# Ordering the column-strip matmuls of the modulation weights: all four of a row tile in a row, the later piece first

## The chip, the cores and the metric

One core of one Trainium2 chip. The metric is device microseconds of one execution of the program; the median of 3 runs of the kernel before is 2380.18 us (2373.62 to 2383.07).

## The reference

Two transformer blocks on 256 tokens of 1024 features, in float32. The first block mixes sparse attention with a gated linear recurrence in chunks and ends with a feed-forward layer. The second has two layers on a sequence x and a context of 256 tokens; each layer scales, shifts and gates its norms and branches by nine modulations, which a vector c (and c_ctx for the context) gives. The change touches these:

```python
for l in range(DEPTH_2):
    mod_x = (jax.nn.silu(c) @ w_ada[l] + b_ada[l]).reshape(bn, 1, N_MOD, d)
    mod_c = (jax.nn.silu(c_ctx) @ w_ada[l] + b_ada[l]).reshape(1, 1, N_MOD, d)
    h_x = _half_ffn(h_x, norm_g[l, 0], mod_x[:, :, 0], mod_x[:, :, 1], mod_x[:, :, 2], ffn1_up[l], ffn1_down[l])
    h_c = _half_ffn(h_c, norm_g[l, 0], mod_c[:, :, 0], mod_c[:, :, 1], mod_c[:, :, 2], ffn1_up[l], ffn1_down[l])
...
```

Here w_ada[l] is 1024 x 9216, and c and c_ctx are one row each.

## The kernel before, in words

Activations lie feature-major (128 features of a tile in the partitions, tokens along the free axis). A large product is three matmuls, because values and weights are split in a high and a low part: `gemm` (L360 to L366) issues high x high (L364), low x high (L365) and high x low (L366) for each row tile. A `Stream` (L333) brings weights in: `load` (L342, its DMA at L349) takes one of a few raw buffers of 128 x 1024 floats (512 KB), `get` (L352) splits such a piece by ScalarE (L356) and by VectorE or GpSimd (L357). All weight loads go through one queue, SP's, which issues them in order and waits when the next one's buffer is still in use. The buffers of a pool are given out in turn, in the order in which the program text asks for them.

The modulations of a layer are made by `Ada.step` (L1150 to L1182) in five parts: four of two modulations each, and one of the last modulation alone. The two vectors (x and context) and 30 zero columns are the stationary operand `sc` of 128 x 32, and the weights are the moving operand, in plain float32. The 1024 rows are eight row tiles (k). In the first four parts a row tile has 2048 columns, which come as two pieces `r` of 1024 columns, and each half of a piece (512 columns) is multiplied by one matmul. Four such matmuls, j = 0 to 3, write four strips of 32 partitions of one PSUM tile, so they use four different groups of 32 columns of the systolic array; j = 0, 1 read the first piece and j = 2, 3 the second:

```python
for j in range(4):
    te.matmul(pt[j * 32:j * 32 + 32], adac[:, k], w[j], start=k == 0, stop=k == KD - 1)   # L1163
if k < KD - 1:
    yield
```

In the fifth part a row tile is one piece of 1024 columns, and a strip has 256 columns. Two layers have 64 row tiles of two pieces and 16 of one, 320 strip matmuls; each shows as two records in the profile (two passes of a float32 matmul). After the eighth row tile four transposes (L1171) and VectorE turn the part into its place.

`step` is a generator: the program takes one row tile at a time between other work. The stream `st_c` with three raw buffers carries the pieces, and it carries also the feed-forward weights of the context in the second block's first layer (`Ffn.group`, L443, which calls `tick` after each hidden tile: two pieces for the gate and up columns, then two modulation pieces), since this part of the context does not wait for block 1 and runs beside it. Block 1 takes ten row tiles ahead of its first norm (`E0`) and then one for each column tile of its projections (L621 on); its own weights come through another stream with two raw buffers. Layer 1's modulations go on beside block 1's output projection and beside the joint feed-forward layers of x and context, after 1200 us, there through three raw buffers of their own.

The order in which instructions stand on an engine is not the order of the program text: the tile framework's scheduler takes, of the instructions that are free by their dependencies, the one that its own model finds ready. So strips of two pieces of a row tile can stand apart, with other matmuls between them, and strips of different row tiles can stand together. Matmuls of one row tile do not depend on each other.

Of the kernel before, what the change touches and what calls it, by code (L numbers as in the profile page):

```python
# [17 lines left out]
PSUM = bass.MemoryType.PSUM  # L18
DRAM = bass.MemoryType.DRAM

D = 1024
KD = 8
# [7 lines left out]
# the work of the three mixers: projections, and then what goes beside the units of either attention (a group for each).  # L30
# q, k, v, c, u: projections; V, C, U: what one of their tiles still needs; b: bias; t: a step from outside; s: statistics
# [106 lines left out]
def stat(w, c0, c1):  # L138
    """[K, M] columns c0:c1 as stationary pieces of 128 columns: [M/128, 128, K/128, 128]."""
    w = np.asarray(w)[:, c0:c1]  # L140
    k, m = w.shape
    return np.ascontiguousarray(w.reshape(k // 128, 128, m // 128, 128).transpose(2, 1, 0, 3))


def movp(w):
    """[1024, 512] as moving pieces of 2 row tiles: [4, 128, 2, 512]."""
    w = np.asarray(w)
    return np.ascontiguousarray(w.reshape(4, 2, 128, w.shape[1]).transpose(0, 2, 1, 3))


def upw(a, b):
    """gate and up columns, interleaved by tile: [22, 2, 128, 8, 128]."""
    return np.ascontiguousarray(np.stack([stat(a, 0, FF), stat(b, 0, FF)], 1))


def per_piece(g):
    """column tiles in a down piece of g row tiles"""
    return 1 if g > 4 else 2 if g > 2 else 4


def dnw(w, groups):
    """[2816, 1024]: for each group of row tiles and few column tiles, [128, g, n * 128], one after another."""
    w = np.asarray(w).reshape(NF, 128, 8, 128)
    out, f0 = [], 0
    for g in groups:
        nd = per_piece(g)
        out.append(np.ascontiguousarray(w[f0:f0 + g].reshape(g, 128, 8 // nd, nd * 128).transpose(2, 1, 0, 3)).ravel())
        f0 += g
    return np.concatenate(out)


def adaw(w):
    """[1024, 9216]: pieces [72, 128, 1024] in the order of their use: two modulations at a time, in four parts"""
    w = np.asarray(w).reshape(8, 128, 9216)
    out = []
    for i in range(4):
        a = w[:, :, i * 2048:(i + 1) * 2048]
        for k in range(8):
            out.append(a[k, :, 0:1024])
            out.append(a[k, :, 1024:])  # L180
    for k in range(8):
        out.append(w[k, :, 8192:])
    return np.ascontiguousarray(np.stack(out))
# [82 lines left out]
def build(tc, A, O, dbg=(), stop=None):  # L266
    nc = tc.nc
    v, s, g, te, sy = nc.vector, nc.scalar, nc.gpsimd, nc.tensor, nc.sync
# [64 lines left out]
    class Stream:  # L333
# [8 lines left out]
        def load(self, src, a, b, i=0):  # L342
            """a piece as it is; other rings than the usual one take the i-th of many at once"""
            if i < self.nr:
                r = tl(self.raw, [128, 1024], tag="r")
            else:
                r = f32(tl((self.h, self.l)[i % 2], [128, 1024], F32R, tag="hl"[i % 2]))
            rv = r[:, 0:a * b].rearrange("p (a b) -> p a b", a=a)
            self.q.dma_start(rv, src)  # L349
            return rv  # L350
# [9 lines left out]
    def gemm(pt, w, m0, m1, xs):  # L360
        """pt += columns m0:m1 of a split stationary piece, over the tiles xs of (hi, lo)"""
        n = len(xs)
        for k in range(n):
            te.matmul(pt, w[0][:, k, m0:m1], xs[k][0], start=k == 0, stop=False)  # L364
            te.matmul(pt, w[0][:, k, m0:m1], xs[k][1], start=False, stop=False)  # L365
            te.matmul(pt, w[1][:, k, m0:m1], xs[k][0], start=False, stop=k == n - 1)  # L366
# [13 lines left out]
    def squares(pp, ps, src, n, late=0, nb=3, scale=None):  # L380
        """sums [128, n / 128] of the squares of src(k), k = 0..7, token-major; the last, late of them, are summed
        by the tensor engine alone"""
        nt = n // 128
        ss = ps(nt)

        def total(sq, first, last):
            for t in range(nt):
                te.matmul(ss[:, t:t + 1], sq[:, t * 128:(t + 1) * 128], ones[:, 0:1], start=first and t == 0, stop=last,
                          skip_group_check=True)

        early = KD - late
        for k in range(KD):
            sq = tl(pp, [128, n], tag="sq", bufs=nb) if k or not early else tl(pp, [128, n], tag="sa", bufs=1)
            s.activation(sq, src(k), AF.Square, scale=scale(k) if scale else 1.0)
            if k == 0:
                acc = sq
            elif k < early:
                g.tensor_tensor(acc, acc, sq, op=OP.add)  # L398
            if k >= early:
                total(sq, k == 0, k == KD - 1)  # L400
            elif k == early - 1:
                total(acc, True, not late)
        return ss

    def stats(pp, ps, src, n, rs, late=0, nb=3):
        """rs [128, n / 128] = 1 / rms of src(k), k = 0..7, token-major"""
# [4 lines left out]
    def rms(pp, ps, src, n, out, late=0, rs=None):  # L411
        """out(k, bc): bc [128, n] is 1 / rms of src(k), k = 0..7, along the columns"""
# [12 lines left out]
    def norm_split(pp, ps, src, n, yh, yl, sc, sh=None, late=0, rs=None):  # L425
        """src * rstd * sc(k) + sh(k) in parts yh, yl"""
# [57 lines left out]
    # ================= block 1 =================  # L484
    def block1(ps, early, ready):
# [8 lines left out]
        # rope tables from the positions  # L494
# [48 lines left out]
        for _ in range(E0):  # L543
            next(early, None)
        with ExitStack() as e:
# [10 lines left out]
            def rope_in(dst, nh, cos, sin, rows=128, pp=pp):  # L556
                """dst [rows, nh, 64] in place"""
# [9 lines left out]
            # token-major queries, then keys and values  # L567
# [57 lines left out]
            # feature-major: receptance, keys, values, low-rank inputs  # L625
# [30 lines left out]
            # compressed keys and values  # L656
# [143 lines left out]
        with ExitStack() as e:  # L800
# [16 lines left out]
            # decay: log w = -e^-0.5 sigmoid(w0 + tanh(w_lat) w2); running sums in each chunk  # L817
# [21 lines left out]
            def head_rstd(sq, scale, eps, floor, neg):  # L839
                """sum of sq over the 64 features of a head -> (.)^-0.5, over the features of the head, in PSUM"""  # L840
# [22 lines left out]
            # negated, normalised keys  # L863
# [15 lines left out]
            # the bonus r . k_mod r_k, over v  # L879
# [9 lines left out]
            # A~ = -kk P_{t-1}, R~ = r P: [pair, token tile, which, token]  # L889
# [20 lines left out]
            # token-major A~, B^, K^, V  # L910
# [20 lines left out]
            # Gram blocks, transposed [j, i]  # L931
# [28 lines left out]
            # (I - L)^-1 by substitution: a partition is (parity of the columns, head, chunk)  # L960
# [92 lines left out]
            # group norm over a head, bonus, gate  # L1053
# [31 lines left out]
    def block1_out(ps, st, before_last):  # L1085
        mix = b1mix
        xr = lambda k: res[:, k, 0:T]
# [1 line left out]
        with ExitStack() as e:  # L1089
# [20 lines left out]
            # the scale of the output norm, and of the norm that follows it on its result  # L1110
# [11 lines left out]
    # ================= block 2 =================  # L1122
# [14 lines left out]
    class Ada:  # L1137
        """modulations of a layer, feature-major: M [128, 9, 8, (x, ctx)], and GS = g (1 + scale) of its three norms"""
# [11 lines left out]
        def step(self, i, st, ps):  # L1150
# [4 lines left out]
            for k in range(KD):  # L1155
# [6 lines left out]
                for j in range(4):  # L1162
                    te.matmul(pt[j * 32:j * 32 + 32], adac[:, k], w[j], start=k == 0, stop=k == KD - 1)  # L1163
# [20 lines left out]
    # each table's rope rows, with the norm's gains (and the queries' 1/8) folded in  # L1184
# [22 lines left out]
    def qkn(pp, src, nh, seg, t, tab, hl):  # L1207
        """heads [128, nh, 64]: norm, rope, split into hl [128, nh, 2, 64]"""
# [80 lines left out]
    def in_v(l, st, pp, ps, yh, yl, segs, kvs, tab):  # L1289
        """values and keys; returns what is left to do for the keys, a token tile at a time"""  # L1290
# [27 lines left out]
    def in_qc(l, st, pp, ps, yh, yl, seg, t0, tab, QC):  # L1318
        """queries; returns what is left to do, a token tile at a time"""
# [24 lines left out]
    def attend(pp, ps, pst, pso, Q, nh, keys, vals, kvof, mh, ml, bias=None, tick=None):  # L1344
        """keys: [(KH, KL)], vals(i, kt, kv) -> [128, 64]; mh, ml [128, nh / 2, 256]"""
# [56 lines left out]
    class Bias:  # L1402
        """the neighbourhoods' bias and mask of (head, token tile) units, in parts, made some units ahead"""
# [22 lines left out]
    def in_u(l, st, pp, ps, yh, yl, c0, mh, ml):  # L1426
        """pooled columns; returns what is left to do, half of the groups at a time"""
# [34 lines left out]
    def mixer(l, seg, st, qp, side, ps, pin, pst, pso, yh, yl, c0, segs, kvs, tab, mixt, orders, out=True, tick=None, extra=None):  # L1462
        """projections of the sequences segs, attention, pooling and output projection of seg; its columns start at c0"""
# [63 lines left out]
    def norm_mod(l, j, seg, pp, ps, yh, yl, late=0, rs=None):  # L1527
        """modulated norm j of a sequence's residual"""
# [12 lines left out]
    def out_proj(l, seg, st, ps, mixt, half):  # L1541
        """one half of the mixed rows, two column tiles a step"""
# [38 lines left out]
    # the context of block 2's first layer does not wait for block 1: its pools lie at the other end of the memory  # L1581
# [53 lines left out]
    # x, first layer  # L1635
# [37 lines left out]
    # both, to the second layer's projections; x goes ahead of the context at each norm  # L1673
# [79 lines left out]
```

## Time and profile before

| | |
|---|---|
| median of 3 runs | 2380.18 us |
| lowest and highest run | 2373.62 and 2383.07 us |
| span of the profiled execution (the only time given for it) | 2382.3 us |
| TensorE, matmuls | 2283.6 us busy, 96% |
| VectorE | 1374.2 us, 58% |
| ScalarE | 946.8 us, 40% |
| GpSimd | 361.0 us, 15% |
| strip matmuls (L1163) | 640 records, in two stretches: 12 to 545 us and 1206 to 1706 us |
| DMA | 376.25 MB, mean 158 GB/s |

The span is the time from the first to the last instruction of one execution that was profiled; the runs are timed without a profile. Busy time is time in which an engine had an instruction in it, whether it could have been shorter or not. A wait names what came last before the waiting instruction could start. In a timeline, equal instructions that follow each other are one line with a count, and the time of a matmul includes its way through the array, so that the next one starts before its end; what a matmul costs is read from the starts.

### The profile page before, as it was taken

How to read it: one execution, taken by the hardware profiler on the slowest of the kernel's cores; microseconds unless marked ns; L12 is line 12 of the kernel's file. 1: busy time of each engine (PE TensorE's matmuls, PEld its weight loads, DVE VectorE, ACT ScalarE, POOL GpSimd, SP SyncE). 2: the span in 40 equal slices, each digit the busy share in tenths (PEclk: the TensorE clock that was granted, in tenths of full speed). 3: DMA queues.
4: the chain of work that ended last, by engine and by line, in shares of the span. 5: the costliest groups of instructions: out<-in, count | busy, mean ns of one | idle time of the engine just before them, and what ended most of it. 6: DMA issues, size and time to landing. Idle time of an engine off the chain costs nothing.

```text
span 2382.3 us, 38350 instructions
## 1 busy us (share of the span) xinstructions
PE 2283.6 (96%) x15317; PEld 1964.1 (82%) x15317; DVE 1374.2 (58%) x2442; ACT 946.8 (40%) x1602; POOL 361.0 (15%) x278
## 2 busy tenths in 40 slices
PE   7999987999999899998999999999999999999998
PEld 3687766888999689997778777798888889778998
DVE  4555566358656766677565333357534347855665
ACT  4334422236444454454543222245322235554443
POOL 2125444444101200002010000011000003200000
PEclk9999998999999899997999999999999999989999
DMA  8865544356554145553166434465523245303554
GB/s 295 283 213 177 177 129 145 108 176 225 181 179 166 62 141 176 174 175 104 41 221 223 159 131 165 138 236 187 195 92 98 92 134 178 116 21 100 185 186 131
DMA packets 114929, 376.25 MB, mean 158 GB/s; under 512 B 18464, under 2 KB 24480, under 8 KB 114752
## 3 DMA queue, kind: packets, MB, share of 16 engines
q1 hardware_dynamic: 114752, 373.82, 47.3%
q8 instruction: 120, 1.97, 0.3%
q14 instruction: 57, 0.47, 0.1%
HBM read 372.20 MB, written 1.57 MB: 157 GB/s over the span
## 4 chain that ended last, share of the span: by engine, by line
PE 65%; issue 23%; DVE 6%; DMA 4%; POOL 1%; ACT 1%; SPq 0%; POOLq 0%; DVEq 0%; ACTq 0%
PE m L364 10%; PE m L366 10%; PE m L365 10%; PE f L364 5%; PE f L366 5%; PE f L365 5%; PE f L1163 3%; DMA r<-in_ada 2%; PE o L1388 2%; PE m L1362 2%; PE f L1378 1%; PE m L1357 1%; POOL sa L398 1%; DVE l L357 1%; ACT h L356 1%
## 5 line engine op out<-in xcount | busy, mean ns | idle before, releaser
L356 ACT CAST h<-r 128x1024 fp32r<-128x1024 f32 (+1 forms) x547 | 567.1, 1042 | 1065.4 <-PE m L365 434.9
L357 DVE TENSOR_TENSOR l<-r,h 128x1024 fp32r<-128x1024 f32 (+1 forms) x467 | 572.3, 1229 | 352.2 <-ACT h L356 343.0
L364 PE MATMUL m<-yh,h 128*128 128x256 f32 (+1 forms) x1624 | 490.2, 303 | 2.3 <-ACT h L356 1.1
L366 PE MATMUL m<-yh,l 128*128 128x256 f32 (+1 forms) x1624 | 489.8, 302 | 1.0 <-DVE l L357 1.0
L365 PE MATMUL m<-yl,h 128*128 128x256 f32 (+1 forms) x1624 | 489.5, 302 | 0.0
L364 PEld LDWEIGHTS m<-yh,h 128*128 128x128 f32 x1624 | 310.1, 192 | 25.9 <-ACT h L356 8.1
L366 PEld LDWEIGHTS m<-yh,l 128*128 128x128 f32 x1624 | 310.2, 191 | 19.8 <-issue 7.1
L365 PEld LDWEIGHTS m<-yl,h 128*128 128x128 f32 x1624 | 310.4, 191 | 15.6 <-issue 3.7
L357 POOL TENSOR_TENSOR l<-r,h 128x1024 fp32r<-128x1024 f32 x80 | 194.2, 2432 | 337.7 <-ACT h L356 318.6
L398 POOL TENSOR_TENSOR sa<-sa,sq 128x256 f32<-128x256 f32 x81 | 86.1, 1064 | 1038.5 <-issue 743.6
L365 PE MATMUL m<-hl,h 128*128 128x256 f32 (+1 forms) x738 | 220.1, 302 | 0.0
L366 PE MATMUL m<-hh,l 128*128 128x256 f32 (+1 forms) x738 | 219.9, 303 | 0.0
L364 PE MATMUL m<-hh,h 128*128 128x256 f32 (+1 forms) x738 | 215.6, 304 | 0.1
L364 PE MATMUL f<-yh,h 128*128 128x256 f32 (+1 forms) x624 | 199.6, 320 | 1.8 <-ACT yh L434 1.1
L365 PE MATMUL f<-yl,h 128*128 128x256 f32 (+1 forms) x624 | 198.0, 317 | 1.2 <-DVE yl L435 1.2
L366 PE MATMUL f<-yh,l 128*128 128x256 f32 (+1 forms) x624 | 197.8, 317 | 0.0
L364 PE MATMUL f<-hh,h 128*128 128x256 f32 (+1 forms) x446 | 138.7, 316 | 14.4 <-DVE ft L461 6.7
L366 PEld LDWEIGHTS m<-hh,l 128*128 128x128 f32 x738 | 139.1, 189 | 8.5 <-issue 1.6
L365 PEld LDWEIGHTS m<-hl,h 128*128 128x128 f32 x738 | 139.7, 189 | 6.7 <-issue 0.4
L364 PEld LDWEIGHTS m<-hh,h 128*128 128x128 f32 x738 | 136.3, 189 | 10.1 <-issue 2.1
L1538 DVE SCALAR_TENSOR_TENSOR res<-m,mod,res 128x256 f32<-128x256 f32 x176 | 79.3, 479 | 111.3 <-PE m L366 111.1
L366 PE MATMUL f<-hh,l 128*128 128x256 f32 (+1 forms) x446 | 135.6, 311 | 1.5 <-POOL l L357 1.5
(509 smaller groups left out, 4120.2 us busy)
## 6 DMA issues: line engine op xcount, KB each, us to landing
r<-in_up SPq DMA_DIRECT2D x252, 512.0 KB, 3.6
r<-in_ada SPq DMA_DIRECT2D x144, 512.0 KB, 4.4
r<-in_dn SPq DMA_DIRECT2D x98, 512.0 KB, 3.6
r<-in_w1u SPq DMA_DIRECT2D x44, 512.0 KB, 3.5
r<-in_dn SPq DMA_DIRECT2D x32, 448.0 KB, 3.3
r<-in_w2m SPq DMA_DIRECT2D x24, 512.0 KB, 4.0
r<-in_w2o SPq DMA_DIRECT2D x24, 512.0 KB, 3.5
r<-in_w1d SPq DMA_DIRECT2D x22, 512.0 KB, 3.5
```

Source lines behind the costliest of these rows:

```text
L356: s.copy(h, r)
L357: self.e.tensor_tensor(l, r, f32(h), op=OP.subtract)
L364: te.matmul(pt, w[0][:, k, m0:m1], xs[k][0], start=k == 0, stop=False)
L365: te.matmul(pt, w[0][:, k, m0:m1], xs[k][1], start=False, stop=False)
L366: te.matmul(pt, w[1][:, k, m0:m1], xs[k][0], start=False, stop=k == n - 1)
L398: g.tensor_tensor(acc, acc, sq, op=OP.add)
L1163: te.matmul(pt[j * 32:j * 32 + 32], adac[:, k], w[j], start=k == 0, stop=k == KD - 1)
L1357: te.matmul(o, q, kh[:, kv], start=True, stop=False)
L1362: te.matmul(o, q[0:64], kl[0:64, kv], start=False, stop=True)
L1378: te.transpose(pT[:, b * 128:b * 128 + 128], P[:, b * 128:b * 128 + 128], ident)
L1388: te.matmul(po[j * 64:j * 64 + 64], vals(b // 2, b % 2, kvof(2 * pr + j)), PT[j][:, b], start=b == 0, stop=b == nt - 1)
L1538: v.scalar_tensor_tensor(r, pt[:, i * T:i * T + T], ad[l].M[:, m, d, q:q + 1], r, op0=OP.mult, op1=OP.add)
```

## The change

The four strip matmuls of a row tile are issued in the order j = 2, 3, 0, 1, and each is tied to the one before it by an order-only dependency. The tie is between instructions of one engine and needs no semaphore; it tells the scheduler that the second must stand after the first. The later piece's strips come first, so what waits for the later load is the first of the four. The rest of the diff removes comments and docstrings; line numbers after the change are higher by 1 up to the edit, and L1163 becomes L1166.

```diff
+NOSYNC = mybir.DependencyInfo(mybir.DependencyClass.NoSync, mybir.DependencyReason.DATA)
...
-                for j in range(4):
-                    te.matmul(pt[j * 32:j * 32 + 32], adac[:, k], w[j], start=k == 0, stop=k == KD - 1)
+                last = None
+                for j in (2, 3, 0, 1):
+                    q = te.matmul(pt[j * 32:j * 32 + 32], adac[:, k], w[j], start=k == 0, stop=k == KD - 1).ins
+                    if last is not None:
+                        tc.add_manual_dep(q, last.name, NOSYNC, reason="strips side by side")
+                    last = q
```

How the order moves, in three places. TensorE before, in block 1's feature-major projections (65 to 140 us of the trace); f_61_235 is the PSUM tile of a part, r_139_586 and r_140_588 are the two pieces of one row tile, and the m tiles are block 1's projections:

```order
L610 MATMUL m_135_566<-cst_1_58,khl_134_561 128x128 x2
L1163 MATMUL f_61_235<-r_139_586,sc_10_82 32x512 x2
L366 MATMUL m_141_594<-yh_66_264,l_138_583 128x256
L364 MATMUL m_141_594<-yh_66_264,h_137_582 128x256
L1163 MATMUL f_61_235<-r_140_588,sc_10_82 32x512 x2
L365 MATMUL m_141_594<-yl_67_265,h_137_582 128x256
```

The two strips of the first piece stand alone, then two matmuls of the projection, then the two strips of the second piece. The same row tile in the order after the change:

```order
L367 MATMUL m_165_729<-yh_66_264,l_162_718 128x256
L1166 MATMUL f_61_235<-r_140_588,sc_10_82 32x512 x2
L1166 MATMUL f_61_235<-r_139_586,sc_10_82 32x512 x2
L365 MATMUL m_165_729<-yh_66_264,h_161_717 128x256
```

All four strips stand in a row, the second piece's first, and later than before: beside the projection's tile m_165 instead of m_141. The next row tile follows after 48 matmuls of the projections.

SP's queue in the same stretch, before; in_ada0 are modulation pieces of layer 0, in_w1s block 1's weights:

```order
L349 DMA r_147_631<-in_ada0 128x1024
L694 DMA wkv2_287_1410<-in_wkv2 128x256
L349 DMA r_148_633<-in_ada0 128x1024
L349 DMA r_155_676<-in_ada0 128x1024
L349 DMA r_156_678<-in_ada0 128x1024
L349 DMA r_176_805<-in_w1s 128x1024
L349 DMA r_163_721<-in_ada0 128x1024
L349 DMA r_186_860<-in_w1s 128x1024
L349 DMA r_164_723<-in_ada0 128x1024
```

And after the change:

```order
L350 DMA r_147_631<-in_ada0 128x1024
L350 DMA r_186_860<-in_w1s 128x1024
L350 DMA r_192_897<-in_w1s 128x1024
L350 DMA r_148_633<-in_ada0 128x1024
L350 DMA r_155_676<-in_ada0 128x1024
L350 DMA r_198_934<-in_w1s 128x1024
L350 DMA r_204_971<-in_w1s 128x1024
L350 DMA r_156_678<-in_ada0 128x1024
L350 DMA r_163_721<-in_ada0 128x1024
```

Two of block 1's loads now stand between one pair of modulation loads and the next; the pair is a row tile's second piece and the next one's first, which take the two buffers that a row tile frees at once.

## Rows read from the trace of the kernel before

**Rows 1.** The page's first part: the span, and busy time by engine.
```profile
span 2382.3 us, 38350 instructions
...
PE 2283.6 (96%) x15317; PEld 1964.1 (82%) x15317; DVE 1374.2 (58%) x2442; ACT 946.8 (40%) x1602; POOL 361.0 (15%) x278
```

**Rows 2.** Windows: stretch, its length, busy us by engine, TensorE clock, DMA share, GB/s.
```profile
0.00:65.00 65.00, 47.88 (x186) 24.40 (x186) 28.29 (x67) 26.43 (x48) 13.49 (x20) 0.95 0.81 290
65.00:140.00 75.00, 73.21 (x532) 58.38 (x531) 46.99 (x93) 31.84 (x55) 7.32 (x22) 1.00 0.79 268
140.00:245.00 105.00, 98.63 (x757) 76.97 (x757) 54.80 (x127) 40.43 (x97) 48.23 (x20) 1.00 0.59 194
245.00:560.00 315.00, 288.46 (x2164) 243.70 (x2163) 183.82 (x355) 100.31 (x162) 145.51 (x85) 0.96 0.47 156
1200.00:1275.00 75.00, 71.20 (x534) 60.15 (x531) 52.52 (x95) 34.34 (x58) 6.67 (x8) 0.98 0.66 226
```

**Rows 3.** Waits of TensorE, 0 to 560 us: total us, times, longest.
```profile
PE m L388 <- POOL sa L398: 10.7, 1, 10.7
...
PE f L364 <- DVE ft L461: 6.7, 1, 6.7
PE f L364 <- DVE res L1538: 5.2, 4, 3.4
PE m L886 <- DVE rk L882: 4.3, 1, 4.3
```

**Rows 4.** The page's chain that ended last, shares of the span by line.
```profile
PE m L364 10%; PE m L366 10%; PE m L365 10%; PE f L364 5%; PE f L366 5%; PE f L365 5%; PE f L1163 3%; DMA r<-in_ada 2%; PE o L1388 2%; PE m L1362 2%; PE f L1378 1%; PE m L1357 1%; POOL sa L398 1%; DVE l L357 1%; ACT h L356 1%
```

**Rows 5.** TensorE's timeline around one piece's strips: start us, us, what, record count.
```profile
74.38 0.28 PE L364 MATMUL m<-yh,h 128*128 128x256 f32 x1
74.59 1.05 PE L1163 MATMUL f<-r,sc 128*32 128x512 f32 x4
75.57 0.39 PE L365 MATMUL m<-yl,h 128*128 128x256 f32 x1
75.79 0.28 PE L366 MATMUL m<-yh,l 128*128 128x256 f32 x1
```

**Rows 6.** The same view where four strips follow each other.
```profile
262.97 0.28 PE L364 MATMUL f<-yhc,h 128*128 128x256 f32 x1
263.09 0.28 PE L365 MATMUL f<-ylc,h 128*128 128x256 f32 x1
263.30 1.07 PE L1163 MATMUL f<-r,sc 128*32 128x512 f32 x8
264.30 0.39 PE L366 MATMUL f<-yhc,l 128*128 128x256 f32 x1
```

**Rows 7.** The same view, six strips in a row.
```profile
525.72 1.91 PE L1163 MATMUL f<-r,sc 128*32 128x512 f32 x12 [0.27 <-DVE res L1538]
527.56 0.39 PE L364 MATMUL m<-mixh,h 128*128 128x256 f32 x1
```

**Rows 8.** The same view, four strips of 256 columns.
```profile
413.61 0.64 PE L1163 MATMUL f<-r,sc 128*32 128x256 f32 x8
414.18 0.38 PE L366 MATMUL f<-yhc,l 128*128 128x256 f32 x1
```

**Rows 9.** TensorE's waits for modulation pieces: whole span, then 65 to 140 us.
```profile
PE f L1163 <- DMA r<-in_ada: 10.3, 9, 3.0
...
PE f L1163 <- DMA r<-in_ada: 1.8, 2, 1.1
```

**Rows 10.** DMA issues, 65 to 140 us: count, KB each, median us to landing.
```profile
r<-in_ada SPq DMA_DIRECT2D x15, 512.0 KB, 4.3
...
l<-in_wv SPq DMA_DIRECT2D x3, 512.0 KB, 6.8
```

**Rows 11.** Waits of SP's queue, 0 to 560 us: total us, times, longest.
```profile
SPq L349 <- PE f L1163: 139.7, 60, 7.6
```

**Rows 12.** TensorE's weight loads in the bunch at 263.30 us.
```profile
263.30 0.16 PEld L1163 LDWEIGHTS f<-r,sc 128*32 128x32 f32 x8
```

## The prediction

> **What bounds the kernel now.** Start with the page's totals: the span is 2382.3 us and TensorE is busy for 96% of it [rows 1]. A busy share says nothing of a stage, so I cut the span where the strip matmuls stand [rows 2]: 0 to 65, 65 to 140, 140 to 245 and 245 to 560 us hold layer 0's modulations and the first of layer 1's, 1200 to 1275 the next ones. TensorE is busy for 73.21 of 75 us in the second of these stretches, for 98.63 of 105 in the third and 71.20 of 75 in the last, but for only 47.88 of 65 in the first and 288.46 of 315 in the fourth. So in the second, third and last stretch a microsecond taken off TensorE should be a microsecond off the end. In the first and the fourth something else ends last part of the time: 10.7 us of start-up and loads in the first, chains of VectorE in the fourth [rows 3]. The chain of waits agrees that strips are on the path: it gives L1163 3% of the span, about 71 us [rows 4].
>
> Then I read what a strip costs. Two strips of one piece that stand alone start at 74.59 and the next matmul starts at 75.57: 0.98 us [rows 5]. Ahead of them the gap is 0.21 us and behind the next matmul 0.22, where matmuls of 256 columns follow each other by 0.12 [rows 5, 6]; so each end of such a bunch costs about 0.1 more, 0.19 together, 1.17 us in all. Four strips side by side take from 263.30 to 264.30, 1.00 us [rows 6]: the second two are all but free. Six strips in a row, where two columns of the array are used twice, take 1.84 us [rows 7]. The unit is thus a round, in which each of the four strips runs at most once: 0.86 us more for each further round, 0.31 for being a bunch at all (0.12 and the 0.19). For row tiles of 256 columns a bunch takes 0.57 [rows 8], 0.76 with its ends, and a further round half of 0.86.
>
> **The change, part by part.** No instruction is added or taken away: the 320 strips (640 records), the 144 loads and the evictions stay, and the tie is between matmuls of one queue, so it costs no semaphore. It moves the strips. I counted bunches and rounds in the order of TensorE's instructions. Tiles of 512 columns: 88 bunches with 93 rounds before, 71 with 71 now, which is one for each of the 64 tiles and 7 more, because six tiles are still cut. Tiles of 256 columns: 16 bunches before, 18 now, 21 rounds in either. That is 17 x 0.31 + 22 x 0.86 = 24.2 us less, and 2 x 0.33 = 0.7 more: 23.5 us less on TensorE. By stretch (bunches and rounds saved):
> 0 to 65 us: 3 and 4, 4.4 us. TensorE is not the limit here; I take half, 2.2.
> 65 to 140 us: 6 and 7, 7.9 us. TensorE's only idle time is 1.8 us for modulation pieces [rows 9], but the transfers ran at 268 GB/s, 0.79 of the DMA engines' time [rows 2], and the same bytes must come in less time. I take 7.
> 140 to 245 us: 4 and 4, 4.7 us. Idle is 6.4 of 105; I take 4.
> 245 to 560 us: 2 and 4, 4.1 us less 0.3 for one more bunch of 256 columns, 3.7 us (rounded). TensorE waits here for VectorE: 6.7, 5.2 and 4.3 us in the largest groups [rows 3]. Those waits stay, and the work that would have filled them is shorter; I take 2.
> 1200 to 1275 us: 2 and 2, 2.3 us, all of it.
> After that: one round, 0.9, less 0.3 for the other bunch of 256 columns: 0.5.
> Sum: 2.2 + 7 + 4 + 2 + 2.3 + 0.5 = 18.0 us.
>
> Against it stands a new wait. Before, the earlier piece's strips ran as soon as it lay there; now all four wait for the later piece, and all matmuls queued behind them wait too. Waiting for modulation pieces cost 10.3 us in 9 waits before [rows 9]. There are now about half as many places to wait, but each waits for the later of two loads. Bounds: 10.3 us less if the later place in the order covers every load; in the other direction 1.1 us, the longest such wait between 65 and 140, in each of the 37 two-piece bunches before 560 us, 41 us. The scheduler put the bunches later: between 65 and 140 us they now stand some 48 matmuls apart, 48 x 0.12 + 1.17 = 6.9 us, and a modulation piece lands 4.3 us after its issue [rows 10]. That is nearer to the low end, and I charge 1 us.
>
> On SP the loads of a pair are issued later: the three raw buffers go round, and now the first buffer of a pair is freed with the second. SP already waited 139.7 us for these matmuls in the first 560 us [rows 11], with the loads of block 1's weights queued behind; the new order puts two of those loads ahead of each pair of modulation loads, so block 1 gains and the context's feed-forward, which shares the buffers, is pushed back: block 1's group norm (L1059) moves from the 2722nd to the 2583rd of TensorE's instructions. I cost that at nothing: the work that hides it is the same context work, run beside block 1's output projection instead. If that cover is gone, the price is a late piece, which is the rival below.
>
> 18.0 - 1.0 = 17.0 us. Against the profiled span that is 2365.3 us. The span is 2.1 us above the median of the three runs, 2380.2, so the forecast on that scale is **2363 us**.
>
> A rule speaks against all this. In the rows eight weight loads of four strips start within 0.16 us at 263.30, while the strips' matmuls are already running [rows 12]. The Trainium skill, "TensorE: Matmul & The Clock Gate", Part 3, says that a weight load overlaps matmuls in flight only where its row group differs; all four strips use the same 128 rows, so by that sentence they would follow each other and the tie would bring little. The trace does not agree.
>
> **The rivals.**
> *Only the saturated stretches pay.* In the first, third and fourth stretch the time is set by loads and VectorE, and between 65 and 140 us by transfers. Then 3 of 7.9 us come out there, 2.3 and 0.5 later, and perhaps 1 elsewhere: 6.8 us, 2373. For it: 0.79 of the DMA time and the waits of rows 3. Against it: TensorE busy for 98% between 65 and 140, and not one wait there but for modulation pieces.
> *More than TensorE's share comes out.* With block 1 earlier in the order, its VectorE chains start earlier and the deferred context work fills the 11 us of the two long waits (6.7 and 4.3): 2353. For it: the context's matmuls are what is left over. Against it: the longest wait is the context's own, for its tile ft behind block 1's work on VectorE.
> *The late piece (slower).* A pair holds two of the three raw buffers, so the later piece of the next pair is issued only when this pair has run. From one bunch to the next there are then at least a load and a bunch, 4.3 + 1.17 = 5.5 us, against the 6.9 us of work between them: 1.4 us to spare. It decides once that load takes over 5.7 us; loads of the same size took 6.8 between 65 and 140 [rows 10]. At 6.8 each of the 37 bunches stalls 1.1 us: 41 - 23.5 gives 17 us more, 2397. For it: SP's long waits. Against it: 6.8 is what a burst of six block 1 loads took, not a modulation piece.
> *The strips do not run side by side in the new order.* Then only ends are saved, 15 bunches x 0.19 = 2.9 us: 2377. Rows 6 stand against it; it is the time that the sentence of the Trainium skill would give.
>
> **How the numbers follow.** Forecast 0.55, saturated stretches alone 0.25, more than the share 0.10, late piece 0.07, no overlap 0.03. No change that a measurement can tell is about 0.5%, 11.9 us, so faster means below 2368.3. Of the forecast's own spread (2356 to 2371) about four fifths lie below it, 0.45; with 0.10 of the second rival and 0.05 of the first, 0.60. Slower by as much is above 2392.1: most of the late piece, 0.05. The rest, 0.35, is the same. The range from 2350 to 2380 holds the forecast, the two rivals beside it and the no-overlap case; it leaves out the late piece and the tails, under 2 in 10.
>
> **What would show it.** In the profile after: bunches of eight records at 1.0 us where pairs of four stood, most of all between 65 and 140 us; some 20 us less busy time on L1163, if the overlap holds; TensorE's total down by about the same; waits for modulation pieces near 10 us. It is wrong if those waits exceed 25 us, if TensorE's idle time grows by what its busy time loses (the first rival), or if strips of one bunch take 1.84 us.

## The result and the profile after

The change makes the kernel slower by half a per cent: 2389.7 us, median of 9 runs (2385.31 to 2404.34), against 2380.44 for the kernel before in the same comparison (9 runs, 2373.62 to 2384.8). The ratio is 1.0052 with a 95% interval of 1.0029 to 1.0074. The forecast was 2363 us, and the range ended at 2380.

The profiled execution of the changed kernel has a span of 2397.8 us, 15.5 more than that of before. It is the third longest of the nine, at a granted clock of 0.962, where the nine run from 0.960 (2403 us) to 0.968 (2386 us). The medians lie 9.3 us apart, so some 6 of the 15.5 us, and part of what the clock costs below, belong to this execution and not to the change. The page's first part and the two rows on strips, which answer to [rows 1, 9]; the second row is from the groups of instructions by line (busy us, mean ns, then idle time ahead):

```profile
span 2397.8 us, 38332 instructions
PE 2281.5 (95%) x15317; PEld 1979.5 (83%) x15317; DVE 1366.8 (57%) x2442; ACT 948.6 (40%) x1602; POOL 355.8 (15%) x278
...
L1166 PE MATMUL f<-r,sc 128*32 128x512 f32 (+1 forms) x640 | 93.3, 596 | 16.1 <-DMA r<-in_ada 16.1
```

The same row of the kernel before, which was not shown so far:

```profile
L1163 PE MATMUL f<-r,sc 128*32 128x512 f32 (+1 forms) x640 | 118.1, 575 | 11.5 <-DMA r<-in_ada 10.3 <-DVE r L513 0.7 <-DVE res L1538 0.3
```

The strips did what the change is for: 118.1 to 93.3 us, 24.8 less. But TensorE's total went from 2283.6 to 2281.5, 2.1 less. The other matmuls, of which there are as many as before, took 22.7 us more, and TensorE's idle time (span less busy time) grew from 98.7 to 116.3, 17.6 more. -24.8 + 22.7 + 17.6 = 15.5: the whole difference of the two spans. The 22.7 agree with the granted clock, whose mean fell from 0.970 to 0.962. With levels at half and at full speed, the time at the half is 2 x (1 - 0.970) x 2382.3 = 143 us before and 2 x (1 - 0.962) x 2397.8 = 182 after; 39 us more at 1.2 GHz in place of 2.4 are some 20 us of lost TensorE time.

Where it is lost, the windows say (the columns of [rows 2]):

```profile
0.00:65.00 65.00, 42.70 (x174) 26.44 (x174) 30.54 (x72) 27.49 (x50) 11.68 (x20) 0.92 0.78 276
65.00:140.00 75.00, 68.54 (x534) 56.58 (x538) 42.90 (x83) 28.79 (x48) 7.29 (x22) 0.95 0.84 293
140.00:245.00 105.00, 95.35 (x735) 79.19 (x728) 53.67 (x129) 40.75 (x99) 42.87 (x18) 0.95 0.47 164
245.00:560.00 315.00, 293.26 (x2141) 250.80 (x2139) 172.51 (x343) 96.84 (x155) 146.15 (x81) 0.94 0.44 151
1200.00:1275.00 75.00, 69.34 (x510) 57.55 (x511) 48.34 (x95) 36.18 (x65) 6.65 (x8) 0.98 0.51 184
```

Read the counts behind TensorE's busy time. Between 65 and 140 us it had 532 records before and has 534 now, although the strips among them are cheaper: the 7 us that I took here did not come out. Busy time fell by 4.7 us (73.21 to 68.54) and the clock from 1.00 to 0.95. Up to 560 us 3639 records ran before and 3584 now.

Which loads come later shows in SP's queue. SP's timeline of the changed kernel (start us, time of the issues, count):

```profile
78.97 0.33 SPq L350 DMA_DIRECT2D r<-in_w1s  x1
80.26 1.18 SPq L350 DMA_DIRECT2D r<-in_ada  x2
83.04 3.20 SPq L350 DMA_DIRECT2D r<-in_w1s  x2
87.20 0.80 SPq L350 DMA_DIRECT2D r<-in_ada  x2
90.57 2.61 SPq L350 DMA_DIRECT2D r<-in_w1s  x2
94.80 0.80 SPq L350 DMA_DIRECT2D r<-in_ada  x2
...
116.79 0.38 SPq L350 DMA_DIRECT2D r<-in_up  x1
```

The kernel before:

```profile
84.21 2.81 SPq L349 DMA_DIRECT2D r<-in_ada  x2
...
90.26 3.65 SPq L349 DMA_DIRECT2D r<-in_ada  x2
...
99.52 0.33 SPq L349 DMA_DIRECT2D r<-in_up  x1
```

Two modulation pieces went out every 6.05 us before (84.21 to 90.26) and go out every 7.27 us now (80.26 to 94.80, two steps). The first feed-forward weight of the context, `in_up`, which stands behind the pieces in the same three buffers, is issued at 116.79 instead of 99.52.

It is not the loads, though, that set this pace. Two of TensorE's bunches, then the windows row of 79 to 123 us and TensorE's waits for modulation pieces in it:

```profile
79.17 1.06 PE L1166 MATMUL f<-r,sc 128*32 128x512 f32 x8
...
86.11 1.06 PE L1166 MATMUL f<-r,sc 128*32 128x512 f32 x8
...
79.00:123.00 44.00, 42.80 (x347) 36.01 (x345) 25.55 (x39) 15.84 (x24) 1.18 (x12) 1.00 0.83 283
...
PE f L1166 <- DMA r<-in_ada: 1.2, 3, 0.6
```

From one bunch to the next are 6.94 us (79.17 to 86.11), in which stand 48 of block 1's matmuls: 48 x 0.12 + 1.17 = 6.93 us of work. Three of the later bunches wait for their piece, 1.2 us in all. So here the order in which the scheduler put the instructions spaces the pairs, and SP follows. Before, from 77 to 104 us, a row tile came after some 30 of block 1's matmuls, about every 6 us. Between 60 and 79 us, where the first bunches have only 6 and 8 matmuls between them, TensorE does wait for the pieces themselves (4.4 us).

TensorE's timeline carries this on. First the kernel before, then the changed one: the context's first feed-forward matmul, block 1's last gate product, the context's last up-projection matmul and the first biased score of x's attention in the second block.

```profile
124.01 0.40 PE L364 MATMUL f<-yhc,h 128*128 128x256 f32 x2
...
509.87 0.28 PE L366 MATMUL f<-yhc,l 128*128 128x256 f32 x1
...
521.59 0.69 PE L1079 MATMUL m<-gl,lora 32*128 32x256 f32 x2
...
1100.81 0.41 PE L1360 MATMUL m<-biash,identr 128*128 128x256 f32 x1
```

```profile
136.71 0.50 PE L365 MATMUL f<-yhc,h 128*128 128x256 f32 x2 [0.21 <-ACT yhc L435]
...
511.00 0.69 PE L1080 MATMUL m<-gl,lora 32*128 32x256 f32 x2
...
528.52 0.28 PE L367 MATMUL f<-yhc,l 128*128 128x256 f32 x1
...
1116.21 0.41 PE L1366 MATMUL m<-biash,identr 128*128 128x256 f32 x1
```

Block 1's gate product comes 10.6 us earlier, the context begins 12.7 later and ends 18.7 later, and x's attention begins 15.4 later, which is already the whole difference of the spans. The end follows the context, not block 1.

### The profile page after: what moved, and what is told of

Read it like the earlier page. It is cut to its first block, busy times and chain, and to the rows that moved or that the text cites. A ratio compares the mean times of both kernels' runs of the same rounds, so it can differ in the third digit from the quotient of the medians.

```text
span 2397.8 us, 38332 instructions
## 1 busy us (share of the span) xinstructions
PE 2281.5 (95%) x15317; PEld 1979.5 (83%) x15317; DVE 1366.8 (57%) x2442; ACT 948.6 (40%) x1602; POOL 355.8 (15%) x278
## 4 chain that ended last, share of the span: by engine, by line
PE 62%; issue 24%; DVE 6%; DMA 5%; POOL 2%; ACT 1%; SPq 0%; POOLq 0%; DVEq 0%; ACTq 0%
PE m L365 9%; PE m L366 9%; PE m L367 9%; PE f L365 5%; PE f L367 5%; PE f L366 5%; PE f L1166 3%; DMA r<-in_ada 2%; PE o L1394 2%; DMA r<-in_up 1%; PE m L1368 1%; PE f L1384 1%; PE m L1363 1%; POOL sa L399 1%; ACT h L357 1%
```

## The experiments

**Theory A, the held buffers.** The first piece of a row tile now keeps its raw buffer until the second has landed. A pair holds two of the three, so the next pair's second load can't start until this pair has run; the scheduler, which builds the order on its own model of the buffers, therefore puts more of block 1's work between pairs. Modulations and context weights come late, work meant to run beside block 1 is left over behind it, and TensorE idles, with its clock lowered, in between. A fourth buffer should bring the forecast gain back. Against it: that the strips' place or the tie is itself the cost; that one stretch or one layer makes the loss; that the deferred work alone makes it, whatever the buffers.

Each ratio is to runs of the kernel before made beside it (medians 2379.87 to 2381.52).

**The changed kernel, and the kernel before, with a fourth buffer.** To make room, the context's first norm gets less scratch (`slim`), in both.

```diff
-    st_c = Stream("sc", 3, 2, side=R, stack=rs, eng=g, parts=rs2)
+    st_c = Stream("sc", 4, 2, side=R, stack=rs, eng=g, parts=rs2)
...
-            sq = tl(pp, [128, n], tag="sq", bufs=nb) if k or not early else ...
+            sq = tl(pp, [128, n], tag="sq", bufs=2 if slim[0] else nb) if k or not early else ...
...
-        dg = tl(pp, [128, n], tag="sq", bufs=3)
+        dg = tl(pp, [128, n], tag="sq", bufs=2 if slim[0] else 3)
...
-            y = tl(pp, [128, n], tag="y1", bufs=3)
+            y = tl(pp, [128, n], tag="y1", bufs=1 if slim[0] else 3)
```

> The changed kernel with a fourth raw buffer for the context's stream (and, to make room for it, fewer scratch buffers in the context's first norm). Theory A, held buffers: issuing the later piece's strips first keeps the first piece's buffer until the second has landed, so two of three buffers are bound, the context's feed-forward weights come later and some 135 of its matmuls are moved behind block 1. With a fourth buffer that hold costs nothing: at least 10 us below e2, near 2362 us, waits of TensorE for modulation pieces under 8 us. Theory B, bunching itself: four strips in a row leave pauses in which the clock falls to half, whatever the ring: no faster than e2, half-clock time still near 200 us. Theory C, block 1's stretch simply pays nothing for TensorE work: within 4 us of e2.

> The kernel before with the same fourth raw buffer and the same smaller norm: the partner of e1. The first piece's buffer was free early before, so theory A expects little of it: within 8 us of the kernel before, 2372 to 2385 us. Theories B and C expect the same.

Measured: the changed kernel with four buffers 2364.86 us (6 runs), ratio 0.9931 (0.9909 to 0.9953); the kernel before with four 2381.14, ratio 0.9984 (0.9967 to 1.0001). So the fourth buffer and the smaller norm together bring the kernel before nothing that can be told, and with them the change is worth 2381.1 - 2364.9 = 16 us, where the forecast had 17. The changed kernel with four buffers is also the fastest version of this study, faster than both kernels.

Its rows, from the same views as above: the page's line of busy times, SP's timeline, two of TensorE's bunches and the four places of the timeline.

```profile
PE 2258.1 (96%) x15317; PEld 1964.9 (83%) x15317; DVE 1380.6 (58%) x2442; ACT 948.0 (40%) x1602; POOL 356.1 (15%) x278
```

```profile
73.05 0.80 SPq L350 DMA_DIRECT2D r<-in_ada  x2
74.28 0.33 SPq L350 DMA_DIRECT2D r<-in_w1s  x1
77.11 0.80 SPq L350 DMA_DIRECT2D r<-in_ada  x2
78.33 0.33 SPq L350 DMA_DIRECT2D r<-in_w1s  x1
81.17 0.80 SPq L350 DMA_DIRECT2D r<-in_ada  x2
82.40 0.33 SPq L350 DMA_DIRECT2D r<-in_w1s  x1
85.23 0.80 SPq L350 DMA_DIRECT2D r<-in_up  x2
```

```profile
76.02 1.07 PE L1168 MATMUL f<-r,sc 128*32 128x512 f32 x8
...
80.08 1.07 PE L1168 MATMUL f<-r,sc 128*32 128x512 f32 x8
```

```profile
112.18 0.40 PE L365 MATMUL f<-yhc,h 128*128 128x256 f32 x2
...
487.02 0.28 PE L367 MATMUL f<-yhc,l 128*128 128x256 f32 x1
...
506.02 0.69 PE L1082 MATMUL m<-gl,lora 32*128 32x256 f32 x2
...
1089.04 0.42 PE L1368 MATMUL m<-biash,identr 128*128 128x256 f32 x1
```

A pair goes out every 4.06 us (73.05, 77.11, 81.17), not every 7.27, and `in_up` at 85.23. Again it is the order that sets this: 24 matmuls now stand between two bunches, and 24 x 0.12 + 1.17 = 4.05. The context's up-projection is 19 us ahead of block 1's gate product, where in the changed kernel with three buffers it is over 17 behind it. In the stretch from 65 to 140 us:

```profile
65.00:140.00 75.00, 70.87 (x587) 62.04 (x588) 50.29 (x87) 32.66 (x56) 11.80 (x24) 0.98 0.74 270
```

587 records, 53 more than in the changed kernel; the kernel before with four buffers has 568 there.

**The tie taken out, the order kept.**

```diff
-                    if last is not None:
+                    if False:
```

> The new issue order 2, 3, 0, 1 without the tie. In the built program all instructions stand on all engines as in the changed kernel, so if the tie adds nothing at run time this is the changed kernel again: 2385 to 2400 us, TensorE work and waits as there. If the tie does cost something at run time, it is nearer to 2380.

Measured: 2394.46 us, ratio 1.0056 (1.0038 to 1.0075), that of the changed kernel. The instructions stand in the same order on all five engines as with the tie; and the tie on the old order, j = 0 to 3, builds the order of the kernel before. So the tie does nothing. In each build the four strips of every row tile stand in the order of the program text, tied or not; they write one PSUM tile, which would explain it. The sentence ahead of the prediction that matmuls of a row tile do not depend on each other is therefore wrong as far as the order goes, as is what is said there of the tie's effect. Asking for the later piece first is the whole change: the first piece's strips can no longer go ahead.

**The new order for one part of the row tiles.** Only for layer 1 (the first diff); only for the first 16 row tiles (the second); for all but those 16 (its reverse, `tie = l == 1 or i >= 2`).

```diff
-                for j in (2, 3, 0, 1):
+                for j in ((2, 3, 0, 1) if l else range(4)):
...
-                    if last is not None:
+                    if last is not None and l:
```

```diff
+                tie = l == 0 and i < 2
-                for j in (2, 3, 0, 1):
+                for j in ((2, 3, 0, 1) if tie else range(4)):
...
-                    if last is not None:
+                    if last is not None and tie:
```

> The new issue order for layer 1's modulations alone; layer 0's keep theirs. Up to block 1's end the instructions then stand as before. Theory A: nothing is lost there, and the two bunches and rounds saved around 1240 us and the single ones behind come out: 2 to 4 us faster than the kernel before, 2377. Theory B: the pauses around 1230 us grow, 2380 to 2385. If more than 5 us are lost here, the loss does not lie beside block 1 at all.

> The new issue order for the first 16 row tiles alone (two parts of layer 0, ahead of and beside block 1's projections, before the context's feed-forward asks for a buffer); all later row tiles as before. Start theory: held buffers make these tiles finish later (122.7 us in the changed kernel, 104.8 before), the context's first feed-forward load stands behind them in the ring of buffers, and so all of the context's work starts some 12 to 17 us late; then most of the loss is here: slower than the kernel before, 2384 to 2394 us, tiles done near 122. Sharing theory: the loss comes where pairs share the buffers with the feed-forward weights; then this one gains its strips, 2370 to 2379.

> The opposite half: the first 16 row tiles as before, the new issue order for all others. Sharing theory: the loss is here, 2385 to 2395 us (in the built order 135 context matmuls stand behind block 1's group norm that stood ahead of it, as in the changed kernel). Start theory: these tiles save 7 to 10 us of TensorE work and lose nothing, 2370 to 2378. If both halves lose, both holds count.

Measured: layer 1 alone 2379.59 us, ratio 0.9993 (0.9979 to 1.0008), no change that can be told, though the 2 to 4 us expected lie within the interval. The first 16 alone 2398.95, ratio 1.0074 (1.0056 to 1.0092). All but these 2405.32, ratio 1.0101 (1.0084 to 1.0119). Both of the last are slower than either theory had said, by 5 and 10 us. TensorE's timeline of the last two, the context's first and last up-projection matmul, first the 16 and then all others:

```profile
137.59 0.51 PE L365 MATMUL f<-yhc,h 128*128 128x256 f32 x2 [0.21 <-ACT yhc L435]
...
524.80 0.28 PE L367 MATMUL f<-yhc,l 128*128 128x256 f32 x1
```

```profile
123.80 0.40 PE L365 MATMUL f<-yhc,h 128*128 128x256 f32 x2
...
536.70 0.28 PE L367 MATMUL f<-yhc,l 128*128 128x256 f32 x1
```

The loss has two places. With the first 16, the context starts 13.6 us late and then runs as long as before (387 us against 386). With the others, it starts on time and takes 413 us. That pairs then hold two of the three buffers that the context's own weights go through would explain it, but isn't shown: with all tiles in the new order it takes 392. Nor do the losses add: 19 and 25 us apart, 9 together (the changed kernel). The strips account for 7.5 of these 35 us: they save 7.9 and 9.4 apart, 24.8 together (busy time 110.2 us with the 16, 108.7 with the others, 93.3 with all). The rest stays open.

**The fourth buffer after 1200 us as well**, `pool("scb", 3, ...)` made 4 on top of the first experiment, for layer 1's modulations there.

> e1 with a fourth raw buffer also for layer 1's modulations after 1200 us. If held buffers cost there too (waits for modulation pieces around 1230 us), 2 to 5 us below e1, 2360 to 2363; if not, e1 again within 2 us.

Measured: 2371.64 us, ratio 0.9965 (0.9954 to 0.9976). It was expected at or below the version with one fourth buffer and is 7 us above it. More buffers are not better everywhere. In its profile TensorE is busy for 13 us more than with one fourth buffer (2271.1) and stands some 25 us longer at half the clock; why the clock fell stays open.

**The smaller norm alone**, three buffers, in the kernel before and in the changed one, since the first experiment changed two things.

> The kernel before with the smaller scratch of the context's first norm that e1 and e2 have, but three raw buffers: the control for that part of them. Strips are as before, but in the built order 72 context matmuls (8.6 us at 0.12) stand behind block 1's group norm that stood ahead of it. Deferral theory: work put behind block 1 costs about its own time, since block 1's stretch is not shortened by it: 4 to 12 us slower than the kernel before, 2385 to 2392. If deferral is harmless and only the strips' pieces matter, 2380 within 3.

> The changed kernel with the same smaller norm and three raw buffers: e1 without its fourth buffer. 192 context matmuls (23 us) are deferred against the kernel before, 57 more than in the changed kernel. Deferral theory: 3 to 10 us slower than the changed kernel, 2393 to 2405, and some 30 to 40 us above e1. If the gain of e1 came from the smaller norm, this is near 2365.

Measured: before with the smaller norm 2393.78 us, ratio 1.0053 (1.0032 to 1.0073); changed with it 2391.08, ratio 1.0046 (1.0029 to 1.0064). The norm costs the kernel before 13 us, a little more than the 4 to 12 expected, and the changed one nothing that can be told. So the gain of the first experiment is the buffer's: on the same norm it takes the changed kernel from 2391.1 to 2364.9, 26 us, and the kernel before from 2393.8 to 2381.1, 13 us. On the same norm the change is worth 16 us with four buffers; with three the difference of 3 is within the noise. Of what the buffer brings, 11 of the 13 us in the kernel before are strips that stand closer together in the new build (busy time 123.0 to 111.9), but only 5 of the 26 in the changed one (94.1 to 89.5).

The kernel before with the smaller norm also shows what late context work costs without the new order. Its `in_up` goes out on time, at 99.21 us, but the context's last up-projection matmul and x's attention come 13.1 and 16.6 us later than in the kernel before:

```profile
523.00 0.28 PE L366 MATMUL f<-yhc,l 128*128 128x256 f32 x1
...
1117.37 0.42 PE L1362 MATMUL m<-biash,identr 128*128 128x256 f32 x1
```

The smaller norm puts 57 more of the context's matmuls behind block 1's group norm (192 against 135), and I had expected the changed kernel to lose by that; it did not. So the price doesn't go by the number. But the traces agree on the sign. Ahead of block 1's group norm stand 1488 of the context's feed-forward matmuls in the kernel before and with layer 1 alone, 1539 in every version with a fourth buffer, and 1296 to 1416 in all others; each of the others is slower than the kernel before, by 9 to 25 us, and none of the rest is.

What TensorE did in each profile, which is one execution (span, busy and strips from the page and the groups by line; idle is span less busy; at half clock is 2 x (1 - clock) x span):

| | span | busy | of it strips | idle | at half clock |
|---|---|---|---|---|---|
| before | 2382.3 | 2283.6 | 118.1 | 98.7 | 143 |
| changed | 2397.8 | 2281.5 | 93.3 | 116.3 | 182 |
| changed, no tie | 2401.9 | 2281.6 | 92.7 | 120.3 | 183 |
| first 16 only | 2398.1 | 2289.8 | 110.2 | 108.3 | 158 |
| all but these | 2405.2 | 2294.8 | 108.7 | 110.4 | 188 |
| before, four buffers | 2379.8 | 2278.7 | 111.9 | 101.1 | 148 |
| changed, four buffers | 2364.2 | 2258.1 | 89.5 | 106.1 | 151 |
| changed, four buffers also after 1200 us | 2372.5 | 2271.1 | 92.2 | 101.4 | 176 |
| layer 1 only | 2375.6 | 2277.2 | 113.9 | 98.4 | 138 |
| before, smaller norm | 2393.5 | 2290.0 | 123.0 | 103.5 | 134 |
| changed, smaller norm | 2382.5 | 2266.9 | 94.1 | 115.6 | 152 |

With four buffers the change takes 22.4 us off the strips, and by the medians 16 come out. With three it takes 24.8 off, and 9 are lost; with three on the smaller norm 28.9, and 3 come out. So three buffers cost some 34 or 26 us against what the strips save, four buffers 6. The last row's profile is of the shortest of its nine executions.

## Why the prediction was wrong

**What a bunch costs: right.** At full clock, bunches of eight records take 1.00 us in the new order too, so [rows 6] carried over and [rows 7] did not come back; a few that met the half clock took up to 1.87. TensorE's timeline of the changed kernel:

```profile
93.71 1.06 PE L1166 MATMUL f<-r,sc 128*32 128x512 f32 x8 [0.59 <-DMA r<-in_ada]
94.70 0.39 PE L365 MATMUL m<-yh,h 128*128 128x256 f32 x1
```

The next matmul starts 0.99 us after the strips. I had some 20 us less on the strips' row, and it shows 24.8. The sentence of the Trainium skill ("TensorE: Matmul & The Clock Gate", Part 3) that weight loads overlap matmuls in flight only across row groups is contradicted here as it was in [rows 12], and the rival that rested on it falls with it.

**"A microsecond taken off TensorE should be a microsecond off the end": failed as I used it.** With three buffers the 24.8 us did not even leave TensorE's busy total: other matmuls took 22.7 longer, at a lower granted clock. Busy for 73.21 of 75 us meant only that there was work at hand in the order as it stood. I took work away and let the rest of the order be, which the new build did not. The rule came near where the modulations were not pushed back: 16 of 22 us with four buffers.

**"I cost that at nothing": the step that failed.** I had seen that the first buffer of a pair is freed with the second, that the context's feed-forward shares the buffers, and that the new order defers it; and I named as cover the same context work beside block 1's output projection. The cover did not do: the context's up-projection ended 18.7 us later, and what stands behind it moved with it, x's attention by 15.4. A fourth buffer, which takes the deferral away, brings 16 of the 17 us forecast; and deferral without the new order costs the kernel before 13 us. I looked at block 1, which did gain, 10.6 us, and took it for the chain that counts. I also asked only for the work that could fill a gap later, not for who waits for the deferred work itself.

**The new wait, 1 us: too small, but not the loss.** Waits for modulation pieces were to be near 10 us, and over 25 would have refuted me:

```profile
PE f L1166 <- DMA r<-in_ada: 16.1, 13, 3.7
```

They are 16.1 us against 10.3 [rows 9], 5.8 more.

**The late piece: near in number, not in mechanism.** The time of 2389.7 lies nearer to this rival's 2397 than to the forecast. It was to decide once a load takes over 5.7 us. DMA issues from 65 to 140 us:

```profile
r<-in_ada SPq DMA_DIRECT2D x17, 512.0 KB, 5.8
```

Modulation pieces now land after 5.8 us, where they took 4.3 [rows 10]; I had used the landing time under the old order for loads that the new order issues in another rhythm. 5.8 + 1.17 is 7.0, which just reaches the 6.9 us of work between bunches. So the limit was touched, but the stalls of 1.1 us at each of 37 bunches did not come: 1.2 us in the stretch of 79 to 123 us, 5.8 more in the whole span. That a pair holds two buffers, the rival's premise, was right; I priced it as stalls of TensorE, and the price showed as a later context and as clock.

**Idle time grows by what busy time loses:** the sign that I set for the first rival. Idle grew by 17.6, though busy time lost 2.1 only. That rival had gain without loss, 2373, and is not what happened. (The second rival's sum is 2352 by its own terms, not 2353.)

**What stays open.** Three buffers act twice: in the scheduler's order and as waits on the chip. From 79 to 123 us it is the order (1.2 us of waits in 44); for the rest of the span the two were not separated. How much a given deferral costs isn't known: 57 matmuls more cost the changed kernel nothing. Nor is the clock shown to be cause or consequence: with four buffers its mean is 0.968 and with the first 16 row tiles alone 0.967, yet the first gains and the second loses, and the kernel before with the smaller norm loses 13 us at 0.972.

## What to carry to other kernels

Putting instructions together so that they run side by side makes all of them wait for the last operand, and every buffer of the earlier ones is held until then: count buffers per group, and give the ring enough that the next group can be loaded while this one waits (here four for groups of two; three lost 9 us and four gained 16). When a change defers work, ask who waits for the deferred work, not only what fills the gap. To see what sets the pace of a group, count the instructions that the built order puts between two of them before blaming a wait: here 48, and 24 with the fourth buffer. A tie is worth testing alone: if the order of the built program is the same without it, it does nothing.

## What the hardware showed that I had not expected

The same 15317 matmul records, with cheaper strips among them, ran with some 39 us more at half the clock, so that TensorE's busy total hardly moved. And loads of one size landed in 5.8 us instead of 4.3 in this stretch. With four buffers the medians are 5.7 in the changed kernel and 6.5 in the kernel before, where it does no harm; so it does not belong to the new order alone, and what sets it was not isolated.
